# Encoder block on one core: second MLP product with sums in kept PSUM banks, weight sums by adding transfers, and a second level of Strassen's scheme in chunks 2 to 4

## The chip, the core and the metric

One core of a Trainium2 chip runs the whole layer as one program. The core has TensorE (PE in the profile; PEld is its weight load), VectorE (DVE), ScalarE (ACT), GpSimd (POOL) and SyncE (SP, which here only issues transfers). The metric is the device time of one execution in microseconds (us); lower is better. Before the change it is 1208.2 us, the median of 3 runs (1207.58 to 1208.48).

## What is computed

The reference is one layer of a bidirectional encoder on 1024 tokens of width 1024, in float32. The change touches only the last line, the second product of the MLP:

```python
def reference(x, norm1_g, w_in, ..., norm2_g, w_mlp_in, w_mlp_out):
    ...
        x = x + merged @ w_o[l]
        h = rms_norm(x, norm2_g[l]) @ w_mlp_in[l]
        x = x + jnp.square(jax.nn.relu(h)) @ w_mlp_out[l]
    return x
```

`w_mlp_out` has 4096 rows and 1024 columns.

## The kernel before

**Precision and Strassen's scheme.** Each float32 operand is scaled by a power of two and split into two float16 parts, a high one (ACT writes it) and a low one (DVE: operand times scale minus high part). A product takes three passes: high by high, high by low, low by high (`PASSES`). Both MLP products use Strassen's scheme in Winograd's form, in which the 2 x 2 block product takes seven products of sums of blocks instead of eight; the sums of blocks are made in float32 before the split.

**Chunks and products.** The second MLP product runs over four chunks `s` of the inner dimension. A chunk has seven products `o` = 0 to 6, so that 28 products `n = 7 * s + o` follow each other; their operands are numbered `i = 16 + n`. The table `ORDER` (L1713) says which of the seven formed blocks of h and which weight block product `o` takes: w11, t2, w21, t3, t1, t4, w22, where t2 is w12 + w22 + w11 (the signs are in the stored weights), t4 is t2 + w21, t1 is w11 + w12 and t3 is w12 + w22. The blocks of h come from DRAM (`HS`, loaded by `h_load` into four turns of `hf`). A product gives 512 tokens by 512 columns. It is done in four units `j` of 128 tokens, each a PSUM bank filled by 12 matmuls of 512 columns (four inner tiles by three passes).

**Preparation.** `prep2(s)` is a Python generator in the list `bg`: each call issues the next few instructions. It first takes the sums of squares of the weights (L1730, L1733, on ACT), makes t2 on POOL (L1739, L1740), and works out the scale: `sum_of` and `scale_of` use a matmul with ones and a chain of tiny DVE instructions ("the scale chain"). Then, for each product, it waits in the order of issue until `pe_done` says that product i - 3 is issued (`gate`), takes one of three operand buffers `OPS[i]`, and issues ACT's high part and DVE's low part of h (L1765, L1767, 2048 elements a partition) and of the weights (L1770, L1776, 1024 elements, twice). After product 0 POOL makes w11 + w12 in place (L1781), after product 1 w12 + w22 (L1785), after product 3 t2 + w21 (L1789). After product 4 the raw weights of the next chunk are loaded and `prep2(s + 1)` joins the list.

**Where results go.** Banks come from `anybank`, which turns through all eight. Products 0, 1 and 3 are added into three accumulators `acc` (chunk 0 by ACT, L1864; later ones by DVE, L1866), the others straight into the result `X1` (DVE, L1875; product 4 into two places). In the last chunk `combine` adds the accumulators to each other and to `X1`, on DVE and POOL, and each finished 128 x 512 block of `X1` is stored.

**What sets the order.** The order of each engine's queue is the order in which the Python code issues: `unit` (L207) issues 12 matmuls, then the eviction `post` of the unit before (`settle`), then calls `step` and `tick` a given number of times (here 2 and 4), and each tick draws one step from the generators. An engine runs its queue in that order; semaphores are added where data needs them. So an eviction of DVE stands behind whatever preparation was issued ahead of it, and a matmul that needs the bank waits for that eviction. The text counts chunks from 1 to 4 (`s` = 0 to 3) and products from 0 to 6.

## Time and profile before

| What | Value |
|---|---|
| Runs, median of 3 | 1208.2 us |
| Profiled execution, span from the first to the last instruction | 1205.3 us |
| Mean granted clock of PE | 1.000 |
| Second MLP product on PE | 911.1 to 1201.3 us |
| PE busy over the span | 99% |
| DVE / ACT / POOL busy over the span | 78% / 63% / 36% |
| Bytes moved by transfers | 173.36 MB, mean 144 GB/s |

The profile is one execution on the chip. A row of a group gives the source line, engine, operation, output and inputs, shape, count, busy time and the mean duration of one, then the engine's idle time just before and what ended it. A row of the timeline gives start, duration, engine, line and operation, with idle time in brackets. Matmuls overlap: what a unit costs is the distance from start to start. The chunks start about 911.1, 983.7, 1056.2 and 1128.8 us.

### The profile page before, as it was taken

The numbers are of one execution on the slowest core, as the hardware profiler recorded it, in microseconds if no ns is written. First come the engines' busy times: TensorE is split into PE (matmuls) and PEld (weight loads), VectorE is DVE, ScalarE is ACT, GpSimd is POOL, SyncE is SP. The second block draws the span as 40 slices with busy tenths as digits, with TensorE's granted clock in tenths as the row PEclk, the third lists the DMA queues.
The fourth block names the chain that finished last, engine by engine and source line by source line (L and its number), as shares of the span: only waits on it lengthen the run. The fifth ranks groups of instructions, "written<-read, shape, count | busy, mean of one in ns | idle before, by whom it ended". The sixth has DMA issues, their size and how long they took to land.

```text
span 1205.3 us, 17076 instructions
## 1 busy us (share of the span) xinstructions
PE 1188.0 (99%) x6294; PEld 573.8 (48%) x6294; DVE 938.7 (78%) x1759; ACT 759.8 (63%) x1183; POOL 433.1 (36%) x280
## 2 busy tenths in 40 slices
PE   6999999999999999999999999999999999999998
PEld 4444445555444444444467444444444444444444
DVE  7777988988368787877878655545548999999997
ACT  7766679867554545337779778678676744746440
POOL 1640011222311112001004465565567471553662
PEclk9999999999999999999999999999999999999999
DMA  7766657676542211224386545445465925334202
GB/s 264 151 213 141 140 119 130 133 146 123 103 123 65 67 56 53 70 93 187 57 155 183 182 159 192 149 139 193 145 247 201 352 97 217 129 138 194 105 35 105
DMA packets 171012, 173.36 MB, mean 144 GB/s; under 512 B 131504, under 2 KB 132016, under 8 KB 166832
## 3 DMA queue, kind: packets, MB, share of 16 engines
q1 hardware_dynamic: 170352, 168.07, 47.9%
q10 hardware_dynamic: 576, 4.19, 0.8%
q8 instruction: 49, 0.80, 0.3%
q14 instruction: 35, 0.29, 0.1%
HBM read 102.51 MB, written 37.75 MB: 116 GB/s over the span
## 4 chain that ended last, share of the span: by engine, by line
PE 73%; DVE 9%; ACT 1%; issue 1%; DMA 1%; DVEq 0%; ACTq 0%
PE ps_d L210 26%; PE ps_s L210 23%; PE ps_o L210 16%; PE ps_d L1039 6%; DVE w_s L1163 2%; PE ps_o L1016 1%; PE ps_s L959 1%; DVE sg L1279 1%; DVE P L999 1%; DMA u2T<-v 1%; DVE sz L973 1%; ACT w_s L1167 0%; DVE sc L317 0%; DVE m L1281 0%; ACT sg L1245 0%
## 5 line engine op out<-in xcount | busy, mean ns | idle before, releaser
L210 PEld LDWEIGHTS <-ops 128*128 128x128 f16 x1356 | 132.4, 98 | 157.3
L210 PEld LDWEIGHTS <-w 128*128 128x128 f16 x1368 | 132.8, 98 | 140.0 <-DMA u2T<-v 0.6
L1039 PE MATMUL ps_d<-uT,w_ws 128*128 128x512 f16 x528 | 123.7, 379 | 0.1
L210 PE MATMUL ps_d<-ops 128*128 128x512 f16 (+1 forms) x528 | 118.3, 374 | 0.0
L1765 ACT ACTIVATE ops<-hf,sc 128x2048 f16<-128x2048 f32 x26 | 52.0, 2000 | 97.9 <-PE ps_o L210 35.2
L210 PE MATMUL ps_s<-ops 128*128 128x512 f16 x492 | 112.9, 379 | 0.0
L1152 POOL TENSOR_TENSOR tsum<-raw 128x512 f32<-128x512 f32 x28 | 46.0, 1658 | 149.6 <-ACT raw L1138 141.6
L1345 POOL TENSOR_TENSOR as<-as 128x512 f32<-128x512 f32 x56 | 77.5, 1384 | 39.3 <-ACT as L1625 36.0
L210 PEld LDWEIGHTS <-w_s 128*128 128x128 f16 x588 | 56.8, 98 | 69.4 <-DVE w_s L1163 1.9
L210 PE MATMUL ps_d<-u2x,w 128*128 128x512 f16 (+1 forms) x360 | 80.0, 372 | 0.0
L210 PEld LDWEIGHTS <-uT 128*128 128x128 f16 x504 | 49.0, 98 | 59.6 <-DMA uT<-u 0.8
L1039 PEld LDWEIGHTS <-w_ws 128*128 128x128 f16 x528 | 51.2, 98 | 54.5 <-DVE cv L861 0.4
L210 PE MATMUL ps_o<-ops 128*128 128x512 f16 x336 | 77.1, 379 | 0.0
L1767 DVE SCALAR_TENSOR_TENSOR ops<-hf,sc,ops 128x2048 f16<-128x2048 f32 x26 | 74.0, 2846 | 3.7 <-ACT ops L1765 3.7
L210 PE MATMUL ps_o<-u2T,w 128*128 128x512 f16 (+1 forms) x324 | 71.7, 371 | 0.0
L1138 ACT ACTIVATE raw<-raw,sc 128x256 f32<-128x256 f32 x172 | 71.0, 493 | 0.8 <-DMA raw<-in_weights 0.7
L1152 POOL TENSOR_TENSOR gsum<-raw 128x512 f32<-128x512 f32 x14 | 19.0, 1376 | 133.0 <-issue 72.8
L1167 ACT ACTIVATE w<-raw,sc 128x512 f16<-128x512 f32 (+1 forms) x28 | 24.6, 927 | 54.1 <-DVE sc L426 54.1
L297 DVE SCALAR_TENSOR_TENSOR w_ws<-raw,sc,w_ws 128x512 f16<-128x512 f32 (+2 forms) x72 | 51.2, 763 | 4.7 <-ACT w_ws L306 4.7
L1658 DVE TENSOR_TENSOR as<-ps_d,as 128x512 f32<-128x512 f32 (+1 forms) x14 | 9.4, 672 | 55.8 <-ACT as L1677 53.4
L210 PE MATMUL ps_s<-u2T,w 128*128 128x512 f16 (+1 forms) x252 | 52.7, 359 | 0.0
L982 ACT ACTIVATE sz<-sz,sc 128x384 f32<-128x384 f32 (+1 forms) x64 | 37.2, 582 | 22.5 <-DVE sc L973 15.0
(357 smaller groups left out, 2629.5 us busy)
## 6 DMA issues: line engine op xcount, KB each, us to landing
raw<-in_weights SPq DMA_DIRECT2D x88, 512.0 KB, 5.4
hs<-as SPq DMA_DIRECT2D x16, 1792.0 KB, 8.7
hf<-hs SPq DMA_DIRECT2D x26, 1024.0 KB, 6.3
w2x<-in_weights SPq DMA_DIRECT2D x16, 512.0 KB, 8.1
raw<-in_weights SPq DMA_DIRECT2D x16, 384.0 KB, 3.5
xt<-in_x SPq DMA_DIRECT2D x8, 512.0 KB, 10.0
gs<-s ACTq DMA_DIRECT2D x4, 1024.0 KB, 4.0
x<-in_x SPq DMA_DIRECT2D x8, 512.0 KB, 9.8
```

The lines of the kernel that those rows point to most:

```text
L210: T.matmul(ps, l, r, start=a, stop=b)
L297: V.scalar_tensor_tensor(lo, self.raw[p][:, o:o + m], sc[:, c:c + 1], hi, op0=OP.mult, op1=OP.subtract)
L959: T.matmul(ps[:, :nb * 128], QD[:, p, e, w, i * 128:(i + 1) * 128], KD[:, 2 * p + e, lo * 128:(lo + nb) * 128], start=w == 0, stop=w == 1)
L982: A.activation(z, z, AF.Exp, scale=-1.0, bias=sc[:, d["mx"]], accum_out=sc[:, d["sm"]])
L1039: T.matmul(ps, l, r, start=a, stop=b)
L1138: A.activation(v, v, AF.Copy, scale=sc[:, at(g, 4 * i + k)])
L1152: G.tensor_tensor(t[:, o], a, b, op=OP.add)
L1163: V.scalar_tensor_tensor(o(1), w, sc[:, s], o(0), op0=OP.mult, op1=OP.subtract)
L1167: A.activation(o(0), w, AF.Copy, scale=sc[:, s])
L1345: sub.tensor_tensor(z[o], z[a], z[b], op=op)
L1765: A.activation(P[:, 1, 0], hf, AF.Copy, scale=sc[:, Rs])
L1767: V.scalar_tensor_tensor(P[:, 1, 1], hf, sc[:, Rs], P[:, 1, 0], op0=OP.mult, op1=OP.subtract)
```

## The change

**Kept banks.** Four of the eight banks (`chain`) belong to the units `j` of products 0, 1, 3 and 5. Product 0 starts a bank, products 1, 3 and 5 add into it without clearing it, and after each of them DVE adds or subtracts the bank's sum so far into its place in `X1` (`PLACE`, with the scale `inv` or its negative `neg`). The accumulators and `combine` are gone. The other four banks (`fixed`) turn for products 2, 4 and 6 and the scale chain's matmul.

**Adding transfers.** In chunks 2 to 4 t2 starts as a second load of w12 from DRAM (two loads of 512 KB) and the sums of weights are transfers issued on POOL's queue that add their source to their destination in SBUF (`accum_op`), each 512 KB; ten in a chunk. Chunk 1 keeps POOL's sums.

**A second level.** In chunks 2 to 4 product 2 (h's block 1 with w21) is split once more: `deep_prep` forms seven blocks of 256 x 256 on either side, in place in `hf` and `w2x`, with sums on POOL and DVE, and splits them into high and low parts in one tile `deep` of its own. `deep_units` does seven sub-products with 2 x 6 matmuls of 256 columns, in pairs, each ahead of one unit of product 3, in three of the `fixed` banks, some of which gather several sub-products. Product 2 needs no gate and no operand buffer.

```diff
@@ -71,14 +71,16 @@
     rc = [0]
+    fixed = []
+
     def anybank():
         rc[0] += 1
-        return bank("dsodsods"[rc[0] % 8])
-
-
-    sc = base.tile([128, 512], F32, name="sc")
+        return fixed[rc[0] % len(fixed)] if fixed else bank("dsodsods"[rc[0] % 8])
+
+
+    sc = base.tile([128, 520], F32, name="sc")
     sci = sc.bitcast(I32)
-    area = {"keep": [0, 0, 144], "prep": [144, 144, 240], "tmp": [240, 240, 512]}
+    area = {"keep": [0, 0, 144], "prep": [144, 144, 240], "tmp": [240, 240, 512], "neg": [512, 512, 520]}
     def cols_of(kind, n):
         a = area[kind]
@@ -204,10 +206,10 @@
         V.tensor_scalar(sc[:, out], bk[:, 0:1], floor, None, op0=OP.max)
         yield
-    def unit(mms, post=None, steps=0, ticks=0):
+    def unit(mms, post=None, steps=0, ticks=0, free=False):
         for ps, l, r, a, b in mms:
-            T.matmul(ps, l, r, start=a, stop=b)
+            T.matmul(ps, l, r, start=a, stop=b, skip_group_check=free)
         units[0] += 1
         work[0] += len(mms) * mms[0][0].shape[-1]
         settle()
@@ -1639,7 +1641,7 @@
             m = tmp()
             V.tensor_reduce(sc[:, m], sc[:, bsum[q // 4]], axis=AX, op=OP.max)
             yield
-            yield from pow2(m, 14, *R[q // 4])
+            yield from pow2(m, 13, *R[q // 4])
             r_ready[q // 4] = True
     def quad(q, c0=0, c1=512):
@@ -1735,9 +1737,25 @@
             yield
         sums = sum_of(sm)
         T2 = later["t2"]()
-        for i in range(2):
-            G.tensor_tensor(T2[:, i], w12[i], w22[i], op=OP.add)
-            G.tensor_tensor(T2[:, i], T2[:, i], w11[i], op=OP.add)
+
+        def add(o, w):
+            for i in range(2):
+                if s == 0:
+                    G.tensor_tensor(o[i], o[i], w[i], op=OP.add)
+                else:
+                    G.dma_start(o[i], w[i], accum_op=OP.add)
+
+        t2 = [T2[:, i] for i in range(2)]
+        if s == 0:
+            for i in range(2):
+                G.tensor_tensor(t2[i], w12[i], w22[i], op=OP.add)
+                G.tensor_tensor(t2[i], t2[i], w11[i], op=OP.add)
+        else:
+            for i in range(2):
+                load_into(t2[i], c2[s], 2 + i)
+            yield
+            add(t2, w22)
+            add(t2, w11)
         yield
         if s == 0:
             yield from gate(17)
@@ -1747,20 +1765,25 @@
         sw, inv = yield from scale_of(sums, 0)
         fw = keep()
         mul(iR, sw, fw)
-        c2[s].inv = inv
+        c2[s].inv, c2[s].neg = inv, cols_of("neg", 1)
+        V.tensor_scalar(sc[:, c2[s].neg], sc[:, inv], -1.0, None, op0=OP.mult)
         yield
         for o, (f, name) in enumerate(ORDER):
             n = 7 * s + o
             i = 16 + n
-            yield from gate(i)
+            if name != "w21" or s not in DEEP:
+                yield from gate(i)
             pool, tag = TAGS[i % 3]
-            if n > 1:
+            if n > 1 and (name != "w21" or s not in DEEP):
                 OPS[i] = pool.tile([128, 2, 2, 2048], F16, name="ops", tag=tag)
-            P = OPS[i]
             while ("h", n) not in later:
                 yield
             if 1 < n < 25:
                 h_load(n + 3)
+            if name == "w21" and s in DEEP:
+                yield from deep_prep(i, later.pop(("h", n)), X2[s][:, 0:2], Rs, fw)
+                continue
+            P = OPS[i]
             hf = later.pop(("h", n)).rearrange("p k t -> p (k t)")
             A.activation(P[:, 1, 0], hf, AF.Copy, scale=sc[:, Rs])
             yield
@@ -1777,16 +1800,15 @@
                 yield
             ready.add(i)
             if name == "w11":
-                for i2 in range(2):
-                    G.tensor_tensor(w11[i2], w11[i2], w12[i2], op=OP.add)
+                add(w11, w12)
                 yield
             elif name == "t2":
-                for i2 in range(2):
-                    G.tensor_tensor(w12[i2], w12[i2], w22[i2], op=OP.add)
+                add(w12, w22)
+                if s in DEEP:
+                    add(t2, w21)
                 yield
-            elif name == "t3":
-                for i2 in range(2):
-                    G.tensor_tensor(T2[:, i2], T2[:, i2], w21[i2], op=OP.add)
+            elif name == "t3" and s not in DEEP:
+                add(t2, w21)
                 yield
             elif name == "t1":
                 done[0] += 4
@@ -1794,6 +1816,103 @@
                 if s < 3:
                     w2x_load(s + 1)
                     bg.append(prep2(s + 1))
+            yield
+
+    DEEP = (1, 2, 3)
+    HSLOT, WSLOT = {0: 0, 1: 1, 3: 2, 5: 3, 6: 4, 2: 5, 4: 6}, {0: 0, 1: 1, 2: 2, 3: 3, 6: 4, 4: 5, 5: 6}
+
+    def deep_prep(i, hf, wx, sh, sw):
+
+        t = OPS[i] = w5p.tile([128, 2, 2, 7, 512], F16, name="deep")
+        w4 = wx.rearrange("p a (k c) -> p (a k) c", c=512)
+        src = [v.rearrange("p k (h c) -> p k h c", h=2) for v in (hf, w4)]
+
+        def todo(m, part):
+            v, o = src[m], t[:, m]
+            if part == 0:
+                return v[:, :, 0], [o[:, w, 0:2].rearrange("p f (k c) -> p (f k) c", k=2) for w in range(2)]
+            if part == 1:
+                return v[:, 2:4, 1], [o[:, w, 2].rearrange("p (k c) -> p k c", k=2) for w in range(2)]
+            return v, [o[:, w, 3:7].rearrange("p f c -> p (f c)").rearrange("p (h k c) -> p k h c", h=2, k=4)
+                       for w in range(2)]
+
+        scale = (sh, sw)
+
+        def hi(m, part):
+            v, o = todo(m, part)
+            A.activation(o[0], v, AF.Copy, scale=sc[:, scale[m]])
+
+        def lo(m, part):
+            v, o = todo(m, part)
+            if part < 2:
+                V.scalar_tensor_tensor(o[1], v, sc[:, scale[m]], o[0], op0=OP.mult, op1=OP.subtract)
+            else:
+                for k in range(4):
+                    V.scalar_tensor_tensor(o[1][:, k], v[:, k], sc[:, scale[m]], o[0][:, k],
+                                           op0=OP.mult, op1=OP.subtract)
+
+        def q(m, h, k):
+            return src[m][:, 2 * k:2 * k + 2, h]
+
+        hi(0, 0), hi(0, 1)
+        yield
+        lo(0, 0), lo(0, 1)
+        yield
+        a, b = (lambda h, k: q(0, h, k)), (lambda k, c: q(1, c, k))
+        G.tensor_tensor(a(0, 0), a(0, 0), a(1, 0), op=OP.subtract)
+        G.tensor_tensor(a(1, 0), a(1, 0), a(1, 1), op=OP.subtract)
+        V.scalar_tensor_tensor(a(1, 1), a(0, 0), -1.0, a(1, 1), op0=OP.mult, op1=OP.subtract)
+        G.tensor_tensor(a(0, 1), a(0, 1), a(1, 1), op=OP.add)
+        yield
+        hi(1, 0), hi(1, 1)
+        yield
+        lo(1, 0)
+        yield
+        lo(1, 1)
+        yield
+        for o, x, y in ((b(0, 0), b(0, 0), b(0, 1)), (b(0, 1), b(0, 1), b(1, 1)), (b(1, 1), b(0, 0), b(1, 1)),
+                        (b(1, 0), b(1, 0), b(1, 1))):
+            V.tensor_tensor(o, x, y, op=OP.add)
+            yield
+        hi(0, 2)
+        yield
+        hi(1, 2)
+        yield
+        lo(0, 2)
+        yield
+        lo(1, 2)
+        ready.add(i)
+        yield
+
+    def deep_units(s):
+
+        t, inv, neg = OPS.pop(16 + 7 * s + 2), c2[s].inv, c2[s].neg
+        banks = {m: anybank() for m in "abc"}
+        seq = {1: ("a", 1, 0, 0, inv), 5: ("c", 1, 1, 1, inv), 2: ("b", 1, 0, 0, inv), 6: ("a", 0, 0, 1, neg),
+               3: ("c", 0, 0, 1, inv), 7: ("a", 0, 1, 1, neg), 4: ("a", 0, 1, 0, inv)}
+
+        def sub(m):
+            bk, fresh, h, c, g = seq[m]
+            ps, (f, w) = banks[bk], SEVEN[m]
+            mms = []
+            for j in range(2):
+                o = ps[:, 256 * j:256 * j + 256]
+                for n, (k, (sa, sw)) in enumerate((k, p) for k in range(2) for p in PASSES):
+                    at_h, at_w = 256 * k + 128 * j, 256 * k
+                    mms.append((o, t[:, 0, sa, HSLOT[f], at_h:at_h + 128], t[:, 1, sw, WSLOT[w], at_w:at_w + 256],
+                                n == 0 and j == 0 and fresh == 1, n == 5))
+
+            def post():
+                x = X1[:, 2 * h:2 * h + 2, 256 * c:256 * c + 256]
+                V.scalar_tensor_tensor(x, ps.rearrange("p (j c) -> p j c", j=2), sc[:, g], x, op0=OP.mult, op1=OP.add)
+                if m == 4 and s == 3:
+                    for r in range(4):
+                        SP.dma_start(out[128 * r:128 * r + 128, :512], X1[:, r, :512])
+            unit(mms, post, 1, 2, True)
+
+        for ms in (1, 5), (2, 6), (3, 7), (4,):
+            for m in ms:
+                sub(m)
             yield
     def first2():
@@ -1820,67 +1939,52 @@
     p4.close()
     p5 = ExitStack()
     w5p = later["pool"] = p5.enter_context(tc.tile_pool(name="p5", bufs=1, reuse_waits="tile"))
-    acc = {i: w5p.tile([128, 4, 512], F32, name=f"acc{i}") for i in (1, 6, 7)}
     t2 = w5p.tile([128, 2, 1024], F32, name="t2")
     later["t2"] = lambda: t2
     later["junk"] = w5p.tile([128, 2048], BF16, name="junk")
-    combined = set()
-    PLACE = {2: ((0, 0),), 4: ((4, 512), (0, 512)), 5: ((4, 0),), 6: ((0, 512),)}
-    SUM = {0: 1, 1: 6, 3: 7}
-
-    def combine(j, o):
...
+    PLACE = {0: ((0, 0, 1),), 1: ((0, 512, 0),), 2: ((0, 0, 1),), 3: ((4, 512, 0),), 4: ((4, 512, 1), (0, 512, 1)),
+             5: ((4, 0, 1),), 6: ((0, 512, 1),)}
+    LAST = {2: (0, 0), 4: (4, 512), 5: (4, 0), 6: (0, 512)}
+    eight = [anybank() for _ in range(8)]
+    chain = eight[:4]
+    fixed[:] = eight[4:]
+
+    def step2(n, j):
+        s, o = n // 7, n % 7
+        P, c = OPS[16 + n], c2[s]
+        bk = chain[j] if o in (0, 1, 3, 5) else anybank()
+        for c0, m in ((0, 256), (256, 256)) if n == 27 and j == 3 else ((0, 512),):
+            ps = bk[:, c0:c0 + m]
+
+            def post(ps=ps, c0=c0, m=m):
+                for b, d, plus in PLACE[o]:
+                    t = X1[:, b + j, d + c0:d + c0 + m]
+                    V.scalar_tensor_tensor(t, ps, sc[:, c.inv if plus else c.neg], t, op0=OP.mult, op1=OP.add)
+                if s == 3 and o in LAST:
+                    b, d = LAST[o]
+                    r = (b + j) * 128
+                    SP.dma_start(out[r:r + 128, d + c0:d + c0 + m], X1[:, b + j, d + c0:d + c0 + m])
+
+            mms = group(ps, [(P[:, 1, sa, 512 * k + 128 * j:512 * k + 128 * j + 128],
+                              P[:, 0, sw, 512 * k + c0:512 * k + c0 + m]) for k in range(4) for sa, sw in PASSES])
+            if o in (0, 1, 3, 5):
+                mms = [(p, l, r, a and o == 0, b) for p, l, r, a, b in mms]
+            unit(mms, post, 2, 4, o in (0, 1, 3, 5))
     for n in range(28):
         s, o = n // 7, n % 7
+        if o == 2 and s in DEEP:
+            continue
         need(16 + n)
...
+        side2 = iter(())
+        if o == 3 and s in DEEP:
+            need(15 + n)
+            side2 = deep_units(s)
         for j in range(4):
+            next(side2, None)
+            step2(n, j)
+        OPS.pop(16 + n)
         pe_done[0] = 17 + n
     settle()
     p5.close()
```

43 lines of the change are left out of this document (removed).

## The prediction

> **What bounds the kernel now.** Read first: the head of the page, then the busy time of each engine in four windows, one for each chunk of the second MLP product (the only part that the diff touches).
>
> ```profile
> PE 1188.0 (99%) x6294; PEld 573.8 (48%) x6294; DVE 938.7 (78%) x1759; ACT 759.8 (63%) x1183; POOL 433.1 (36%) x280
> ...
> 911.10:983.70 72.60, 72.60 (x339) 32.91 (x338) 63.99 (x59) 50.50 (x50) 41.83 (x15) 1.00 0.64 239
> 983.70:1056.20 72.50, 72.50 (x338) 32.88 (x337) 69.43 (x63) 37.51 (x33) 33.38 (x11) 1.00 0.43 158
> ...
> 1128.80:1201.30 72.50, 72.50 (x349) 33.89 (x347) 68.58 (x63) 20.41 (x15) 36.20 (x17) 1.00 0.21 80
> ```
>
> The columns after a window are its length and the busy time of PE, PEld, DVE, ACT and POOL, then granted clock, DMA share and GB/s. PE is busy the whole window at clock 1.00: every microsecond that PE gains or waits here is a microsecond of the kernel. DVE, at 64 to 69 of 72.5 us, is close behind. The timeline of PE says what one unit (12 matmuls into one bank) takes, and when the chunk's first two products start:
>
> ```profile
> 911.12 2.75 PE L210 MATMUL ps_s<-ops 128*128 128x512 f16 x12
> 913.71 2.75 PE L210 MATMUL ps_o<-ops 128*128 128x512 f16 x12
> ...
> 921.48 2.75 PE L210 MATMUL ps_d<-ops 128*128 128x512 f16 x12
> ...
> 654.36 1.47 PE L210 MATMUL ps_d<-u2x,mH 128*128 128x256 f16 x12
> 655.67 1.47 PE L210 MATMUL ps_s<-u2x,raw 128*128 128x256 f16 x12
> ```
>
> Start to start, a unit of 512 columns takes 913.71 - 911.12 = 2.59 us, one of 256 columns 1.31. A product is four units, 10.36 us; product 1 of chunk 1 starts at 921.48.
>
> **The matmuls removed.** In chunks 2 to 4 product P2's four units of 512 columns become seven sub-products of 12 matmuls with 256 columns: 7 x 1.31 = 9.17 us for 10.36, 1.19 less, times 3: **-3.6 us**. That is all the gain on the path that sets the end.
>
> **DVE's work.** Its pace where nothing disturbs it, and where POOL adds at the same time:
>
> ```profile
> 1002.28 2.34 DVE L1767 SCALAR_TENSOR_TENSOR ops<-hf,sc,ops 128x2048 f16<-128x2048 f32 x1
> 1004.54 2.47 DVE L1776 SCALAR_TENSOR_TENSOR ops<-raw,sc,ops 128x1024 f16<-128x1024 f32 x2
> 1006.93 0.74 DVE L1866 SCALAR_TENSOR_TENSOR acc<-ps_o,sc,acc 128x512 f32<-128x512 f32 x1
> 1007.59 0.74 DVE L1866 SCALAR_TENSOR_TENSOR acc<-ps_d,sc,acc 128x512 f32<-128x512 f32 x1
> ...
> 1030.79 6.68 DVE L1776 SCALAR_TENSOR_TENSOR ops<-w2x,sc,ops 128x1024 f16<-128x1024 f32 x2
> ...
> 881.46 5.33 POOL L1345 TENSOR_TENSOR as<-as 128x512 f32<-128x512 f32 x4 [12.72 <-ACT as L1625]
> ```
>
> A low part of h costs 2.26 us, the two of a weight 2.39, an eviction 0.66. Beside POOL's sums the pair takes 6.68, so the sums that become transfers give DVE back up to 4.2 us a pair. A chunk with a second level then asks of DVE: six ordinary products 6 x 4.65 = 27.9; the second level's low parts, 2 x 3584 elements, and five sums of 512 at 0.6 each (half of 1.2): 8.4 + 3.0; 28 + 7 evictions 23.1; the scale chain 1. That is 63.4 of PE's 71.3 us. On the average DVE is not the bound, and the relief is worth nothing by itself: PE never waited for DVE. What counts is where DVE is late.
>
> **The kept banks, chunk 1.** Before, eight banks rotated, and products 0, 1 and 3 of chunk 1 went to their accumulators by ACT. Now product 1 adds into the four banks of product 0, so its first matmul waits until DVE has read bank 0 into x1. In the changed program's order that read is queued behind both low parts of product 2's weights. In the trace of before that stretch of DVE's queue is:
>
> ```profile
> 921.13 2.34 DVE L1767 SCALAR_TENSOR_TENSOR ops<-hf,sc,ops 128x2048 f16<-128x2048 f32 x1
> 926.82 0.16 DVE L1640 TENSOR_REDUCE sc<-sc 128x1 f32<-128x4 f32 x1 [3.35 <-ACT as L1625]
> 927.08 2.13 DVE L1776 SCALAR_TENSOR_TENSOR ops<-w2x,sc,ops 128x1024 f16<-128x1024 f32 x1
> ...
> 929.20 2.23 DVE L1776 SCALAR_TENSOR_TENSOR ops<-w2x,sc,ops 128x1024 f16<-128x1024 f32 x1
> 931.35 0.14 DVE L112 TENSOR_SCALAR sc<-sc 128x1 int32<-128x1 int32 x1
> ...
> 918.78 2.00 ACT L1765 ACTIVATE ops<-hf,sc 128x2048 f16<-128x2048 f32 x1 [4.21 <-DMA hf<-hs]
> ...
> 924.69 2.00 ACT L1625 ACTIVATE as<-as,sc 128x2048 f32<-128x2048 f32 x1
> ```
>
> Nothing ahead of it is changed: ACT starts after the load of h, squares the last quad of the first MLP product, DVE's maximum waits for that until 926.82, and the low parts end at 931.35. The read follows, 0.74 us, and PE goes on at about 932.1 where it wants 921.48: **+10.6 us**. The other three reads follow at 0.66 each, while PE takes 2.59 a unit, so it waits once.
>
> **The second level's preparation, chunks 2 to 4.** I walk DVE's queue as the changed program orders it, with zero where product 5 of the chunk ahead ends on PE. Product 6 then runs to 10.4, product 0 to 20.7, product 1 should start there. Chunk 3: the scale chain ends at 3.9 (product 6's first unit ends at 2.6, its eviction at 3.4, four scalars follow); then low parts of product 0 and evictions to 9.9; of product 1 to 14.5; eviction 15.2; second level, h, first 1536 elements 1.8 us to 17.0; bank 0 of product 0 read at 17.7; two dependent sums on POOL (5.33 / 4 = 1.33 each) end at 19.7, DVE's own sum at 20.3; second level, weight 22.1; bank 1 read 22.8; four sums of weights 25.2; bank 2 read 25.8; eight low parts of 512, 4.8 us, 30.6; bank 3 read 31.3. PE wants bank 3 at 28.5: a wait of 2.8. Behind it stand product 3's low parts (35.9), four evictions and product 4's h (40.8), then the read of the first sub-product (41.5), whose bank the fourth sub-product wants at 40.4: 1.1 more. Chunk 4 has the same order: 3.9 us each. In chunk 2 product 0's low parts come one eviction earlier; its walk has bank 0 at 20.8 and bank 1, behind the eight low parts, at 26.3 where PE wants 23.4: 3.0. Together **+10.8 us**.
>
> **The adding transfers.** No such transfer is in the trace; the nearest are plain ones:
>
> ```profile
> w2x<-in_weights SPq DMA_DIRECT2D x12, 512.0 KB, 7.7
> raw<-in_weights SPq DMA_DIRECT2D x11, 512.0 KB, 5.7
> out_y<-x SPq DMA_DIRECT2D x15, 256.0 KB, 2.1
> out_y<-x SPq DMA_DIRECT2D x2, 128.0 KB, 1.7
> ```
>
> (KB each, us to landing.) 128 KB more cost 0.4 us, so 512 KB alone take some 2.9, a pair 4.5; in a crowd 7.7. Each is issued on POOL's queue, in order, and the next pair waits where it needs the one before. Three pairs (w11, w12, then t2 with w21) stand between product 0's low parts (9.2) and DVE's in-place sums of w21 (22.8), which must not start before t2 has read w21; behind them on DVE stand the reads for which PE waits. At 4.5 a pair the last lands at 22.7: nothing. At 7.7 it lands at 32.3, 9.5 us late in each chunk, 28.5 in all. Below nothing it can't go: the reads stay where they are. I take 3 us a chunk, nearer to the low end because the DMA share of these windows is under one half: **+9 us**. The load of t2 and its two adding pairs, 5.7 + 2 x 7.7 = 21.1 us, fit the 23 us between product 5's low part (-15.3) and ACT's use (8); the first pair's slack is 2 us, so POOL's issue time isn't free either.
>
> The Trainium skill (DMA: Bandwidth & Descriptors, "Anatomy of one DMA — SWDGE (gpsimd) path") gives 2.0 us plus bytes over 436 GB/s for a transfer issued there: 3.2 us for 512 KB, an estimate by that page; no run here shows one, and by it this term would be 0 to 1 us a chunk.
>
> **Edits at nothing.** The constant 13 for 14, the wider sc and one more tensor_scalar a chunk (0.15 us as the rows of scalars show). Gone in chunk 4 are 12 sums on POOL and 12 on DVE; evictions of chunk 1 move from ACT to DVE, where the walk has them. SP gets two more loads of 512 KB a chunk. The end itself stays: the last bank in two halves, evicted and stored.
>
> ```profile
> 1198.69 2.78 PE L210 MATMUL ps_d<-ops 128*128 128x256 f16 x24
> 1201.51 0.88 DVE L1875 SCALAR_TENSOR_TENSOR x<-ps_d,sc,x 128x256 f32<-128x256 f32 x2 [1.87 <-PE ps_d L210]
> ```
>
> **Sum:** -3.6 + 10.6 + 10.8 + 9 = +26.8. The profiled span is 1205.3 us, the median of the runs 1208.2, so 2.9 lie around the span; after: span 1232, run **1235 us**, 2.2% slower.
>
> **Rivals.** (a) *Only the first chunk waits.* DVE without POOL's sums reaches the later reads in time: 1208.2 - 3.6 + 10.6 = 1215.2. For it: 6.68 us against 2.47 for the same pair. Against it: the walk already uses the quick pace, and its waits come from the order. (b) *The transfers decide.* Pairs at 7.7 us: 1208.2 + 17.8 + 28.5 = 1254.5. For it: three pairs in a row on one queue; against it: little else moves then. (c) *Twice that*, because a destination is read and written: 3 x 15.4 against 13.6 us of room, 32.6 late a chunk, 98 in all: 1324. (d) *Not slower:* the reads of the kept banks are done before PE asks, in chunk 1 before 921.48, because ACT's square and the low parts of product 2 come 10.6 us sooner, and DVE keeps ahead later for the same reason: 1208.2 - 3.6 = 1204.6. It decides as soon as bank 0 is free within the four units of product 0. For it: POOL's sums slowed the low parts at 929 to 931; against it: only 2 of the 10.6 us are such slowing, the rest is a load and ACT.
>
> The Trainium skill (SBUF — State Buffer, "Who interferes with whom") has the port pair that VectorE and GpSimd share as an exclusive lock, and descriptors that GpSimd writes held up while VectorE has it; the 6.68 us row agrees with the lock. Held-up descriptors would be a cause of (b).
>
> **How the numbers follow.** Forecast 0.56, with a range of its own of 1222 to 1246; (a) 0.14, (b) 0.17, (c) 0.06, (d) 0.07. The range 1214 to 1268 takes in (a) and (b) and leaves out (c), (d) and little of the rest. 0.2% is 2.4 us, about what can be told from no change: faster has (d)'s chance but for 0.01, 0.06; same 0.02, a mix of (a) and (d); slower 0.92.
>
> **What would show it.** In the profile after: PE with idle time of some 10 us before the first matmul of product 1 in chunk 1, released by DVE's eviction; about 3 to 7 us before product 1 in each of chunks 2 to 4, released by the same line; units of the second level 1.31 us apart; adding transfers of 3 to 8 us on POOL's queue. PE without a gap near 921 would break the largest term; gaps of over 15 us ahead of product 1 in chunks 2 to 4, with DVE waiting for a transfer, would mean (b) or (c).

## The result, and the profile after

| What | Before | After |
|---|---|---|
| Runs, median | 1207.9 us (4 runs, 1207.0 to 1208.5) | 1253.7 us (4 runs, 1251.6 to 1254.7) |
| Profiled execution, span | 1205.3 us | 1252.0 us |
| Mean granted clock of PE | 1.000 | 0.985 |
| Second MLP product, units of product 0 of chunk 1 to the end | 911 to 1201 us | 911 to 1248 us |
| POOL busy | 433 us | 349 us |

The changed kernel is slower: ratio 1.038, 95% interval 1.0365 to 1.0394. The forecast was 1235 with a range of 1214 to 1268; the time lies inside the range, 19 us above the forecast. The span has grown by 46.7 us, and all the rows below are about where these went.

First the head of the page of the changed kernel: PE's busy time, and PE and its granted clock in 40 slices of 31 us (a 9 is 90% or more).

```profile
PE 1195.5 (95%) x6402; PEld 586.1 (47%) x6402; DVE 926.4 (74%) x1814; ACT 761.5 (61%) x1180; POOL 348.9 (28%) x277
...
PE   6999999999999999999999999999969979979798
...
PEclk9999999999999999999999999999979989989899
```

Before, PE was full in every slice but the first and the last. Now it has holes in the last quarter, and, which the prediction had not thought of, the clock dips in the same slices. PE's busy time is 7.5 us longer although 3 x 1.19 us of matmuls were taken out. Next the waits of PE from 900 us on (what it waited for: us in total, times, longest):

```profile
PE ps_o L212 <- DVE x L1963: 15.6, 3, 7.2
PE ps_s L212 <- DVE x L1963: 11.1, 3, 8.1
PE ps_s L212 <- issue: 10.9, 1, 10.9
PE ps_s L212 <- DVE x L1907: 1.5, 2, 0.7
```

L1963 is DVE's eviction, and in these rows the read of a kept bank; L1907 is the eviction of a sub-product. Together 39.1 us: 10.9 in chunk 1 (the row with "issue" is that one; the timeline shows below that it too ends with the read), 28.2 in chunks 2 to 4. The timeline of PE shows where they stand, here in chunks 1 and 3 (start, duration, in brackets the idle time before and what ended it):

```profile
932.41 5.19 PE L212 MATMUL ps_s<-ops 128*128 128x512 f16 x12 [10.90 <-issue]
937.44 2.75 PE L212 MATMUL ps_o<-ops 128*128 128x512 f16 x12
...
1100.07 4.99 PE L212 MATMUL ps_o<-ops 128*128 128x512 f16 x12 [7.08 <-DVE x L1963]
1104.90 2.75 PE L212 MATMUL ps_d<-ops 128*128 128x512 f16 x12
1109.47 2.75 PE L212 MATMUL ps_s<-ops 128*128 128x512 f16 x12 [1.82 <-DVE x L1963]
...
1119.68 1.47 PE L212 MATMUL ps_s<-deep 128*128 128x256 f16 x12 [0.74 <-DVE x L1907]
```

In chunk 1 product 1's first unit starts 10.9 us late; in chunk 3 (and in chunk 4) its first unit is on time and the second one, which adds into the second kept bank (ps_o), starts 7.1 us late. And the first unit behind each of these waits takes 937.44 - 932.41 = 5.03 and 1104.90 - 1100.07 = 4.83 us in place of 2.59. The same units with their granted clock (windows of the trace; the column after POOL's is the clock):

```profile
932.41:937.44 5.03, 5.03 (x12) 1.73 (x13) 5.03 (x5) 0.00 (x0) 4.95 (x4) 0.51 0.43 160
937.44:942.60 5.16, 5.16 (x25) 2.35 (x24) 5.16 (x3) 0.00 (x0) 3.34 (x1) 1.00 1.05 306
```

Twelve matmuls at clock 0.51 behind the wait, then 1.00 again. In chunks 2 to 4 the unit behind the long wait takes 4.56, 4.83 and 5.07 us, so the four cost 2.44 + 1.97 + 2.24 + 2.48 = 9.1 us more than full speed. Sum: -3.6 + 39.1 + 9.1 = 44.6 of the 46.7 us. Of the other 2.1 us, 1.3 are in the way of counting: a wait counts from the end of a unit, 2.75 us after its start, while a unit without a wait costs 2.59, which makes 0.16 for each of eight waits. 0.4 is in the second unit of chunk 4 (3.14 us in place of 2.75), and 0.4 at two sub-products.

What DVE does ahead of the read in chunk 1 is as forecast:

```profile
927.05 0.16 DVE L1642 TENSOR_REDUCE sc<-sc 128x1 f32<-128x4 f32 x1 [3.65 <-ACT as L1627]
...
929.43 2.22 DVE L1799 SCALAR_TENSOR_TENSOR ops<-w2x,sc,ops 128x1024 f16<-128x1024 f32 x1
...
931.58 0.74 DVE L1963 SCALAR_TENSOR_TENSOR x<-ps_s,sc,x 128x512 f32<-128x512 f32 x1
```

The read ends at 932.32, PE goes on at 932.41. In chunk 3 the order on DVE is the forecast one too, but it holds a wait that the forecast didn't have. DVE's waits for POOL in the three chunks (us in total, times, longest), and DVE's timeline in chunk 3:

```profile
DVE hf L1864 <- POOL hf L1863: 26.0, 3, 8.8
```

```profile
1086.45 0.75 DVE L1963 SCALAR_TENSOR_TENSOR x<-ps_s,sc,x 128x512 f32<-128x512 f32 x1
1095.81 0.69 DVE L1864 SCALAR_TENSOR_TENSOR hf<-hf 128x512 f32<-128x512 f32 x1 [8.61 <-POOL hf L1863]
...
1099.28 0.74 DVE L1963 SCALAR_TENSOR_TENSOR x<-ps_o,sc,x 128x512 f32<-128x512 f32 x1
```

and POOL's in the same stretch, where DMA_DIRECT2D is the issue of an adding transfer:

```profile
1083.57 0.86 POOL L1746 DMA_DIRECT2D raw<-w2x  x1 [3.59 <-DMA raw<-raw]
1087.77 0.86 POOL L1746 DMA_DIRECT2D raw<-w2x  x1 [3.34 <-DMA raw<-raw]
1088.38 1.17 POOL L1746 DMA_DIRECT2D t<-w2x  x1
1092.27 0.87 POOL L1746 DMA_DIRECT2D t<-w2x  x1 [2.72 <-issue]
1092.83 1.60 POOL L1862 TENSOR_TENSOR hf<-hf 128x512 f32<-128x512 f32 x1
1094.51 1.26 POOL L1863 TENSOR_TENSOR hf<-hf 128x512 f32<-128x512 f32 x1
```

POOL has two short sums of h to make, L1862 and L1863, and DVE stands 8.6 us for them, from 1087.2 to 1095.8. The sums themselves take 2.9 of these. They are late because they stand behind the issues: those of raw<-w2x had waited 3.59 and 3.34 us for raw<-raw to land, and the last issue of t<-w2x was held another 2.72 us, for which the trace names no cause. The bank that PE wants at about 1093.0 is read from 1099.28 on, behind DVE's sum.

### The profile page after: what moved, and what is told of

It reads as the page before. It is cut to its first block, busy times and chain, and to the rows that moved or that the text cites. A ratio compares the mean times of both kernels' runs of the same rounds, so it can differ in the third digit from the quotient of the medians.

```text
span 1252.0 us, 17392 instructions
## 1 busy us (share of the span) xinstructions
PE 1195.5 (95%) x6402; PEld 586.1 (47%) x6402; DVE 926.4 (74%) x1814; ACT 761.5 (61%) x1180; POOL 348.9 (28%) x277
## 4 chain that ended last, share of the span: by engine, by line
PE 45%; DVE 11%; issue 8%; DMA 6%; POOL 4%; ACT 2%; SPq 0%; POOLq 0%; DVEq 0%; ACTq 0%
PE ps_d L212 18%; PE ps_s L212 16%; PE ps_o L212 11%; DMA t<-in_weights 2%; DVE w_s L1165 2%; DMA t<-raw 1%; DVE ops L1790 1%; DMA raw<-raw 1%; DVE deep L1851 1%; POOL as L1347 1%; DMA hf<-hs 1%; POOL t L1746 1%; DVE x L1963 1%; DVE sg L1281 1%; DMA u2T<-v 1%
## 5 line engine op out<-in xcount | busy, mean ns | idle before, releaser
L212 PEld LDWEIGHTS <-ops 128*128 128x128 f16 x1212 | 120.2, 100 | 184.4 <-issue 53.1
L212 PE MATMUL ps_s<-ops 128*128 128x512 f16 x492 | 116.3, 389 | 22.0 <-DVE x L1963 11.1
L1788 ACT ACTIVATE ops<-hf,sc 128x2048 f16<-128x2048 f32 x23 | 45.8, 1993 | 83.7 <-PE ps_s L212 57.2
L212 PE MATMUL ps_d<-ops 128*128 128x512 f16 (+1 forms) x420 | 93.5, 374 | 0.0
L212 PE MATMUL ps_o<-ops 128*128 128x512 f16 x300 | 73.6, 398 | 15.6 <-DVE x L1963 15.6
L1790 DVE SCALAR_TENSOR_TENSOR ops<-hf,sc,ops 128x2048 f16<-128x2048 f32 x23 | 55.7, 2422 | 5.2 <-ACT ops L1788 5.2
```

Source lines behind the costliest of these rows:

```text
L212: T.matmul(ps, l, r, start=a, stop=b, skip_group_check=free)
L1788: A.activation(P[:, 1, 0], hf, AF.Copy, scale=sc[:, Rs])
L1790: V.scalar_tensor_tensor(P[:, 1, 1], hf, sc[:, Rs], P[:, 1, 0], op0=OP.mult, op1=OP.subtract)
```

## The experiments

All times are device medians; the kernel before was run beside each group, with 1207.5, 1206.9, 1207.6 and 1207.5 us in the four. All kernels in the table compute the whole layer.

| Run | What differs | us | ratio to before (95%) |
|---|---|---|---|
| after | the change | 1253.7 | 1.038 (1.0365 to 1.0394) |
| e_first_read | chunk 1: reads ahead of product 2's low parts | 1248.0 | 1.0332 (1.0317 to 1.0348) |
| e_no_second | no second level | 1220.3 | 1.0101 (1.0084 to 1.0118) |
| e_h_sums_dve | sums of h on DVE | 1247.1 | 1.0326 (1.031 to 1.0341) |
| e_w21_dram | t2 + w21 taken from DRAM, later | 1242.3 | 1.0282 (1.0266 to 1.0297) |
| e_w21_h | the last two together | 1232.2 | 1.0225 (1.0198 to 1.0252) |
| e_reads_no_second | no second level, reads of chunk 1 first | 1208.4 | 1.0011 (1.0002 to 1.002) |
| e_h_early | all repairs, half for h early | 1214.9 | 1.0067 (1.0052 to 1.0082) |
| e_pool_sums | weight sums on POOL again | 1267.0 | 1.0496 (1.0481 to 1.0512) |
| e_paced | e_h_early with the rest later | 1206.1 | 0.9989 (0.998 to 0.9998) |
| e_paced_evenly | e_paced with other pauses | 1206.9 | 0.9995 (0.9986 to 1.0004) |
| e_waits_a, e_waits_b | e_reads_no_second with idle sums on DVE | 1219.0, 1226.6 | 1.0095 (1.008 to 1.011), 1.016 (1.0143 to 1.0177) |

**Chunk 1's wait.** The low part of product 2's h, and with it that of its weights, waits in chunk 1 until product 1's first unit is issued, so the four reads are queued ahead of it.

```diff
+            while i == 18 and units[0] < start5[0] + 5:
+                yield
             V.scalar_tensor_tensor(P[:, 1, 1], hf, sc[:, Rs], P[:, 1, 0], op0=OP.mult, op1=OP.subtract)
```

> Edit: in chunk 1 the low parts of product 2 are issued behind the eviction of product 0's units, so that DVE reads the kept banks first. Theory (the order of DVE's queue makes the wait): the 10.9 us wait ahead of product 1 in chunk 1 goes, and with it the slow unit behind it (5.03 us for 2.59): 13.3 us less, 1240.5, at most some 5 us of it given back because chunk 2 is reached sooner than its weights: 1240 to 1246. Rival (DVE has too much to do and the backlog only moves on): 1249 or more, with a wait as long in chunk 1's later products.

It took 1248.0 us, a gain of 5.8, between the expected 1240 to 1246 and the rival's 1249, so neither came out. PE's wait in chunk 1 fell from 10.9 to 4.1 us and not to nothing. DVE's timeline in that run says why:

```profile
926.15 0.16 DVE L1642 TENSOR_REDUCE sc<-sc 128x1 f32<-128x4 f32 x1 [3.25 <-ACT as L1627]
...
926.60 0.74 DVE L1965 SCALAR_TENSOR_TENSOR x<-ps_s,sc,x 128x512 f32<-128x512 f32 x1
```

L1642 is the maximum over the last quad of the first MLP product, and it waits 3.3 us for ACT's square. Its result is the scale of h in chunk 4, but the read stood behind it. The unit after the 4.1 us still took 5.07 us, so almost nothing of the slow start was saved either.

**The second level as a whole.** It is left out of all chunks (product 2 is an ordinary product again); kept banks and transfers stay.

```diff
-    DEEP = (1, 2, 3)
+    DEEP = ()
```

> Edit: no second level, product 2 is ordinary in all chunks; kept banks and adding transfers stay. Theory (the long waits of chunks 2 to 4 come from the second level's preparation; chunk 1's wait from the kept banks): only chunk 1's 13.3 us stay against the kernel before: 1221, no wait of over 1 us in chunks 2 to 4. Rival (kept banks or the adding transfers by themselves hold PE in every chunk): waits of 5 us or more ahead of product 1 in chunks 2 to 4, 1235 or more.

1220.3 us, as expected of the theory: the second level costs 1253.7 - 1220.3 = 33.4 us net of the matmuls it saves, and what is left, 12.8 us over before, is one wait of PE of 10.1 us in chunk 1 and the slow unit behind it (5.07 us). To settle that nothing else is in it, the edit of e_first_read was added to this kernel, and the reads were put ahead of the maximum too:

```diff
+            while q == 15 and units[0] < start5[0] + 7:
+                yield
             m = tmp()
             V.tensor_reduce(sc[:, m], sc[:, bsum[q // 4]], axis=AX, op=OP.max)
```

> Kept banks and adding transfers without the second level, and in chunk 1 the reads of the kept banks are put ahead of product 2's low parts and ahead of the maximum over the last quad of the first MLP product, whose queue place made DVE wait 3.3 us for ACT in the run with early reads alone. Theory 1 (without the second level the only cost is chunk 1's wait of 10.1 us and the slow unit behind it): 1207 to 1210.5 us, about the time of the kernel before; DVE's low parts of product 1 end at about 922.9, so PE waits some 1 us there. Rival (kept banks or adding transfers cost something elsewhere as well): 1213 us or more, with a wait of PE in chunks 2 to 4.

1208.4 us, PE waiting 0.3 us in the whole second product. With the reads in that place, kept banks and adding transfers by themselves are within 0.2% of the kernel before, and chunk 1's wait 1220.3 - 1208.4 = 11.9 us.

**What DVE waits for in chunks 2 to 4.** Two suspects stand in POOL's queue: the sums of h, behind the transfers, and the transfers themselves, one of which (t2 + w21) must have read w21 before DVE may change it. Each was taken away alone. First the three sums of h, from POOL to DVE:

```diff
-        G.tensor_tensor(a(0, 0), a(0, 0), a(1, 0), op=OP.subtract)
-        G.tensor_tensor(a(1, 0), a(1, 0), a(1, 1), op=OP.subtract)
+        V.tensor_tensor(a(0, 0), a(0, 0), a(1, 0), op=OP.subtract)
+        V.tensor_tensor(a(1, 0), a(1, 0), a(1, 1), op=OP.subtract)
         V.scalar_tensor_tensor(a(1, 1), a(0, 0), -1.0, a(1, 1), op0=OP.mult, op1=OP.subtract)
-        G.tensor_tensor(a(0, 1), a(0, 1), a(1, 1), op=OP.add)
+        V.tensor_tensor(a(0, 1), a(0, 1), a(1, 1), op=OP.add)
```

> Edit: the three sums of h's blocks at the second level move from POOL to DVE. Theory (two things are late one behind the other: POOL's sums, which stand behind the transfers in POOL's queue, and the transfer that reads w21, which lands about when DVE's sums of w21 begin now): DVE's 8.6 us wait for POOL goes, but most of it comes back ahead of the sums of w21: 1243 to 1254. Rival (only POOL's queue is late): 7.2 + 2.3 us less in each of three chunks, 1225.

1247.1 us, 6.7 less. DVE's longest sum of waits is now another one (L1875 are the in-place sums of w21):

```profile
DVE w2x L1875 <- DMA t<-w2x: 16.9, 6, 4.6
```

The wait for POOL, 26.0 us in the changed kernel, is gone, and 16.9 us of waiting for the transfer that reads w21 have come out from under it. Then the other one alone: the sum of t2 with w21 reads w21 from DRAM, where DVE doesn't change it, and is issued after product 3's split.

```diff
             elif name == "t3":
-                if s in DEEP:
-                    add(t2, w21)
+                if s in DEEP:
+                    for i2 in range(2):
+                        G.dma_start(t2[i2], bass.AP(tensor=weights.tensor, offset=weights.offset + c2x[s].offs[i2],
+                                                    ap=[[1024, 128], [1, 1024]]), accum_op=OP.add)
```

> Edit: w21 is added to t2 from DRAM, after product 3's split, so that no transfer reads the w21 that DVE changes in place and two transfers fewer stand ahead of POOL's sums of h. Theory (order of POOL's queue and the wait for w21): the waits ahead of product 1 in chunks 2 to 4 shrink from about 9 to 3 to 4 us, and the slow unit behind each goes: some 7.5 us less in each, 1231, within 5. Rival (the adding transfers are slow by themselves, or DVE is): the same 9 us of waits, 1250 or more.

1242.3 us, between the two expected numbers. POOL's sums of h are now behind two transfers fewer, but still behind w12 + w22, and DVE's waits say so (first the wait that is left in this run):

```profile
DVE hf L1867 <- POOL hf L1866: 10.7, 3, 4.1
```

**Both together.**

> Both edits on POOL's queue together: the sum of t2 with w21 reads w21 from DRAM and is issued after product 3's split, and the three sums of h are made by DVE. With the first alone (1242.3 us) DVE still waited 10.7 us in all, in 3 places, for POOL's sum of h. Theory 1 (the waits ahead of product 1 in chunks 2 to 4 are DVE's reads queued behind preparation that itself waits for POOL): most of these 10.7 us go, less some 2 us a chunk that the sums now cost DVE: 1231 to 1238 us. Rival (DVE's own work ahead of the reads is what lasts; POOL is only late beside it): no gain over 1242.3, so 1241 to 1247 us, the same waits at the same places.

1232.2 us (1231.7 to 1238.3), inside the expected 1231 to 1238: 6.7 and 11.5 us alone, 21.6 together. PE's waits alone don't explain that the two make more than their sum: they fell by 5.0 and 12.4 us, and by 16.7 together. The rest lies in the slow units: alone, four were left in either kernel (7.5 and 8.3 us over full speed, 9.1 in the changed kernel), together two (3.9 us), since two of the three waits of 3.1 to 3.2 us here were followed by units of full speed. PE's waits in this run:

```profile
PE ps_s L212 <- issue: 10.9, 1, 10.9
PE ps_s L212 <- DVE x L1966: 6.9, 3, 3.2
PE ps_o L212 <- DVE x L1966: 3.1, 1, 3.1
PE ps_d L212 <- DVE x L1966: 0.8, 2, 0.4
PE ps_s L212 <- DVE x L1910: 0.7, 1, 0.7
```

Chunk 1's is as before; chunks 2 to 4 have 6.9 + 3.1 + 0.8 + 0.7 = 11.5 us left. That is what DVE's own order costs when it waits neither for POOL nor for a transfer.

**Transfers or POOL.** The reverse test: the weight sums of chunks 2 to 4 go back to POOL, with the second level in place.

```diff
-                if s == 0:
-                    G.tensor_tensor(o[i], o[i], w[i], op=OP.add)
-                else:
-                    G.dma_start(o[i], w[i], accum_op=OP.add)
+                G.tensor_tensor(o[i], o[i], w[i], op=OP.add)
```

> The changed kernel with the weight sums on POOL in all chunks, as before the change, in place of the adding transfers. Theory 1 (what delays DVE is that POOL's sums of h stand behind the weight sums in POOL's queue, and a pair of sums on POOL takes longer, 5.3 us and more, than issuing its two transfers): the wait of DVE for POOL's sum of h grows from 8.6 us, and DVE is slowed beside POOL as well: 1260 to 1285 us. Rival (the landing of the adding transfers, 7.2 us in the median, is the delay): faster than the changed kernel, 1230 to 1248 us.

1267.0 us, in the expected interval, though only one half of the reason came true. DVE's wait for POOL's sum of h didn't grow; it fell from 26.0 to 12.4 us in all, where no landing of a transfer stands in POOL's queue. DVE beside POOL is slower, as its timeline in chunk 3 shows, and is busy 960.6 us in this run, 926.4 in the changed kernel:

```profile
1087.13 6.65 DVE L1796 SCALAR_TENSOR_TENSOR ops<-t,sc,ops 128x1024 f16<-128x1024 f32 x2
...
1094.36 5.45 DVE L1845 SCALAR_TENSOR_TENSOR deep<-hf,sc,deep 128x1024 f16<-128x1024 f32 x2
```

The same two rows of the changed kernel:

```profile
1081.54 2.48 DVE L1799 SCALAR_TENSOR_TENSOR ops<-t,sc,ops 128x1024 f16<-128x1024 f32 x2
...
1084.59 1.94 DVE L1848 SCALAR_TENSOR_TENSOR deep<-hf,sc,deep 128x1024 f16<-128x1024 f32 x2
```

The pair takes 6.65 us beside POOL's sums and 2.48 beside the transfers, the other 5.45 and 1.94. So the transfers do what they are for, and replacing POOL's sums is worth 13.3 us in this kernel.

**A version without the waits.** DVE has nothing to do while the scale chain waits; the second level's half for h needs no scale of the weights. It is issued there, at most three steps of it, with the repairs above:

```diff
+            if r == WAIT and s in DEEP and taken < 3:
+                taken += 1
+                advance(side_h)
```

> All repairs together: early reads in chunk 1 as in the kernel without the second level, w21 for t2 from DRAM, the sums of h on DVE, and the second level's half for h issued up to three steps while the scale chain still waits (DVE has nothing else there), with the remaining low parts cut in two. Theory 1 (the second level costs by its place in DVE's queue, not by its amount): waits ahead of product 1 in chunks 2 to 4 of at most 5 us each and no slow units behind the short ones: 1206 to 1216 us. Rival (DVE has too little time in these chunks, so the waits only move): 1225 us or more.

1214.9 us, inside the expected 1206 to 1216. The largest part of what is left, about half of it, is one wait of 3.0 us in chunk 2 with its slow unit, which was not expected behind so short a wait. DVE's timeline there, and behind it PE's:

```profile
987.92 0.75 DVE L1991 SCALAR_TENSOR_TENSOR x<-ps_o,sc,x 128x512 f32<-128x512 f32 x1
...
995.01 2.14 DVE L1905 TENSOR_TENSOR w2x<-w2x 128x512 f32<-128x512 f32 x3
997.06 0.74 DVE L1991 SCALAR_TENSOR_TENSOR x<-ps_s,sc,x 128x512 f32<-128x512 f32 x1
```

```profile
997.95 4.27 PE L212 MATMUL ps_s<-ops 128*128 128x512 f16 x12 [3.01 <-DVE x L1991]
1002.67 2.75 PE L212 MATMUL ps_o<-ops 128*128 128x512 f16 x12 [0.45 <-DVE x L1991]
```

The eviction at 987.92 belongs to a unit that PE had finished by 979.4: DVE's evictions run many microseconds behind, because preparation that isn't due yet (the sums of w21 are for sub-products that start at 1010) is issued between them. So that half is issued later, and the sub-products that gather in one bank are set further apart:

```diff
+        for _ in range(4):
+            yield
         hi(1, 0), hi(1, 1)
...
         hi(1, 2)
         yield
+        for _ in range(8):
+            yield
...
-        for ms in (1, 5), (2, 6), (3, 7), (4,):
+        for ms in (1, 5), (2,), (6, 3), (7,), (4,):
```

> The kernel with the second level's half for h early (1214.9 us), and two things more. The weights' half of the second level is issued later: four steps of pause ahead of it and eight ahead of its last low parts, so that DVE's reads of product 0's kept banks are queued ahead of it (in that kernel they still ran up to 12 us behind PE). And the sub-products go 1 and 5, 2, 6 and 3, 7, then 4 behind product 3's last unit, so that two that gather in one bank are further apart. Theory 1 (only queue places are left, 9 us of waits and slow units): PE waits under 1 us in chunks 2 to 4, and the 3.6 us of matmuls saved show: 1204 to 1207 us, 1 to 4 below the kernel without the second level (1208.4). Rival (DVE at some 68 of 71 us a chunk has no room left, waits move to products 3 to 6): 1210 us or more.

> As the run before, with pauses of four steps at each of three places: ahead of the weights' half, ahead of its sums, and ahead of its last low parts. Theory 1: the same, 1204 to 1207.5 us; which of the two is shorter isn't foreseen within 1 us. Rival (no room left on DVE): 1210 us or more, with waits of PE ahead of product 3 where the later preparation ends too late.

1206.1 us for the first, inside the expected 1204 to 1207, and 1.5 below the kernel before beside it: ratio 0.9989, 0.998 to 0.9998, a gain at the edge of what can be told. The second, with its pauses spread evenly, took 1206.9 us, also as expected, and can't be told from before (0.9995, 0.9986 to 1.0004). First the head of e_paced's page, then PE's waits in it:

```profile
PE 1184.3 (98%) x6402; PEld 583.8 (48%) x6402; DVE 927.4 (77%) x1823; ACT 761.3 (63%) x1180; POOL 338.9 (28%) x268
```

```profile
PE ps_s L212 <- DVE x L1995: 1.0, 1, 1.0
PE ps_s L212 <- issue: 0.3, 1, 0.3
```

With 1.3 us of waits left, PE's busy time is 3.7 us below the 1188.0 of before: the matmuls saved, at last to be seen.

**The slow unit by itself.** In the kernel without the second level, idle sums of 512 were put on DVE ahead of the first read of product 0's banks in chunks 2 to 4 (4, 6 and 11 of them in one kernel, 5, 8 and 16 in the other).

```diff
+                if o == 0 and j == 0:
+                    for k in range(EXTRA.get(s, 0)):
+                        V.tensor_tensor(idle[:, 1 + k % 3], idle[:, 0], idle[:, 0], op=OP.add)
```

> A measurement of the slow unit by itself: the kernel without the second level (1208.4 us, no wait of PE over 0.3 us), with 4, 6 and 11 idle sums of 512 on DVE (0.66 us each) ahead of the first read of product 0's banks in chunks 2, 3 and 4. That read ended at 993.7 in chunk 2, and PE wants the bank at 994.1, so PE should wait some 2.3, 3.6 and 6.9 us, with nothing of the second level there. Theory 1 (a wait of PE of some 3 us or more is itself followed by a unit of 12 matmuls that takes 4.2 to 5.2 us in place of 2.6): the unit behind the first wait is normal, those behind the second and third are slow; time 1208.4 + 12.8 + about 4.5 = 1225.7. Rival (the slow units come of what else ran in those kernels, the adding transfers late in the chunk or DVE's and ACT's work on the second level): units of 2.6 us behind all three, 1221 us.

> As the run before, with 5, 8 and 16 idle sums: waits of some 3.0, 4.9 and 10.2 us. Theory 1: slow units behind the second and third at least, and the third costs no more than the second (one unit, about 2.4 us), so 1208.4 + 18.1 + 5 to 7 = 1231.5 to 1233.5. Rival (no slow unit without the second level): 1226.5 us; or, if the slowing grows with the wait, more than one slow unit behind the 10.2 us.

The waits came out shorter than planned, and with them the times (1219.0 and 1226.6). Clearing the idle sums' tile (1.76 us of DVE) stood ahead of the read in chunk 1 and made PE wait 2.4 us there, with a slow unit behind it; PE came that much later to the next chunks, so that part of the delay made for them fell into this room. The times alone therefore decide nothing, although they lie near the rival's 1221 and 1226.5; the unit behind each wait does. In e_waits_a the wait in chunk 4 was 3.88 us and the unit behind it took 3.85; in e_waits_b a wait of 2.08 us in chunk 3 was followed by a unit of full speed. In e_waits_b, PE's timeline and its clock in chunk 4:

```profile
1153.59 4.76 PE L212 MATMUL ps_s<-ops 128*128 128x512 f16 x12 [6.89 <-DVE x L1973]
1158.18 2.75 PE L212 MATMUL ps_o<-ops 128*128 128x512 f16 x12
```

```profile
1153.59:1158.18 4.59, 4.59 (x12) 1.62 (x13) 4.59 (x5) 0.00 (x0) 0.00 (x0) 0.55 0.00 0
1158.18:1163.30 5.12, 5.12 (x25) 2.35 (x24) 3.29 (x4) 0.00 (x0) 0.00 (x0) 1.00 0.00 0
```

A slow unit at clock 0.55 with no second level, no transfer in flight (the last two columns, DMA share and GB/s, are 0) and ACT and POOL idle: the rival, that the slowness comes of what else ran, falls. One unit is slow, and the next at full clock.

## Why the prediction was right in kind and 19 us short

In the span the forecast is 46.7 - 26.8 = 19.9 us short: 9.1 in slow units, 7.7 in the term of the transfers, 0.3 in chunk 1 and 0.7 in DVE's walk, and the 2.1 us of small things above.

**The matmuls, -3.6: right.** The sub-products start 1.31 us apart, and where the waits are gone the 3.7 us show in PE's busy time.

**Chunk 1, +10.6: right, with its mechanism.** The wait was 10.9 us; the read came at 931.58 where the working had 931.35. Undone by moving the read in DVE's queue, it gave back 11.9 in the kernel without the second level; what the term lacked is the slow unit behind the wait.

**DVE's walk in chunks 2 to 4, +10.8: right as an account of DVE's own queue.** With POOL and the transfers out of its way PE's waits there are 11.5 us. Chunk for chunk they are 3.6, 3.6 and 4.3 (the waits over 0.3 us in that run's timeline), the walk had 3.0, 3.9 and 3.9. The places agree too: 3.1 us ahead of the second kept bank in chunk 2 and 3.2 ahead of the fourth in chunks 3 and 4, as the walk had them.

**The adding transfers, +9: the mechanism right, the size too small, and one place missed.** Waits of 28.2 us in chunks 2 to 4 less the 11.5 of DVE's own order leave 16.7 us where the term had 9. The mechanism that was priced, DVE's in-place sums waiting until the transfer has read w21, is real: with POOL's sums out of the way it made DVE wait 16.9 us, 5.6 a chunk, between the ends 0 and 9.5 and above the 3 taken. The step that failed is the sentence in the walk "two dependent sums on POOL (5.33 / 4 = 1.33 each) end at 19.7". They cost 1.6 and 1.3 us, near the price, but they were taken to start when DVE was ready, while the change puts the issues of w11 + w12, w12 + w22 and t2 + w21 ahead of them in POOL's queue. With the walk's zero at 1069.52 in chunk 3, where product 6 starts on PE, DVE's read of bank 0 ends at 17.7, as forecast; POOL's second sum ends at 26.2 and not at 19.7. Of what held the queue, the trace names the landing of raw<-raw for the second pair; for the last issue of the third pair, held 2.7 to 4.0 us a chunk, it names nothing, so that part of the cause stays open (us in total, times, longest):

```profile
POOL t L1746 <- issue: 10.1, 3, 4.0
```

The landing was dearer than the low end of the bounds, too. The issues of the second product after (KB each, median us to landing):

```profile
t<-w2x POOLq DMA_DIRECT2D x12, 512.0 KB, 7.3
t<-raw POOLq DMA_DIRECT2D x6, 512.0 KB, 4.8
raw<-raw POOLq DMA_DIRECT2D x6, 512.0 KB, 6.2
raw<-w2x POOLq DMA_DIRECT2D x6, 512.0 KB, 8.1
```

The three kinds that stand ahead of the sums of h (6.2, 8.1 and 7.3) are nearer to the 7.7 us of the crowd than to the 4.5 of the quiet pair; only t<-raw, earlier in the chunk, is not. The Trainium skill (DMA: Bandwidth & Descriptors, "Anatomy of one DMA — SWDGE (gpsimd) path") would give 3.2 us each; the trace doesn't agree for these adding transfers.

**Slow units, not in the sum: 9.1 us.** The prediction took a wait as its length. Behind each of four waits of 7 us and more the next unit took 2.0 to 2.5 us longer, at a granted clock of 0.51 in the one shown above. This is the largest single part of the error, and no term of the sum stood for it. The Trainium skill (TensorE: Matmul & The Clock Gate, "Part 1: The HAM clock gate (the "warmup" mystery)") has the rule: half clock after an idle window of about 3.4 us, full again after as long of work, with windows that run freely. The trace agrees in the halving (0.51) and in one unit being slow. By the Trainium skill's figures, an estimate, 1.7 us (half of 3.4) would have been added to the forecast for chunk 1's wait, the only one that it put above 3.4 us at a stretch.

**Edits at nothing.** SP's additional loads and the longer scale chain cost nothing that can be seen: the kernel with all of them and no second level takes 1208.4. But "the relief is worth nothing by itself" can hold only for the order before; in the changed order POOL's sums cost 13.3 us more. The exclusive lock that the prediction took from the Trainium skill (SBUF — State Buffer, "Who interferes with whom") agrees with the 6.65 us against 2.48; the held-up descriptors that it named as a cause of (b) were not seen: an issue took 0.85 to 1.2 us, and through all three of the longer holds DVE stood idle.

**The rivals.** (b), the transfers decide, named 1254.5 and the run took 1253.7, but the agreement is partly chance: beside the 17.8 us that it shares with the forecast (18.8 measured), it had 28.5 us of landings alone, while the runs show 16.7 for landings and POOL's queue together, 9.1 for the clock and 2.1 of small things. (a) fell with the 28.2 us of waits in chunks 2 to 4, (c) with transfers of 4.8 to 8.1 us in the median, (d) with the read at 931.58. From 1253.7 to 1206.1 the steps of the runs are 21.6 us (POOL's queue and w21), then 17.3 (chunk 1's reads and the half for h early, not tried one by one in that kernel), then 8.8 (the rest later).

## What to carry to other kernels

Short work that another engine waits for must not be queued behind instructions that wait for a transfer; look in each queue for what stands ahead of it, also on an engine that is idle most of the time. Where banks are kept, the reads become part of PE's path: issue preparation that isn't due behind them, and price a wait of PE of more than about 2 us at its length plus a slow unit. A wait can hide under another: when DVE's 26.0 us of waiting for POOL were taken away, 16.9 us of waiting for a transfer came out, so take both away before calling either cheap.

## What the runs showed of the hardware that was not expected

**The clock after a wait.** In the second MLP product of all profiled executions of this study, 23 units of 12 matmuls of 512 columns came behind a wait of PE of 3.88 us or more, and all took 3.8 to 5.3 us in place of 2.59. Behind waits of 2.1 us or less none was slower than 2.75. Between 2.2 and 3.3 us both are found, 8 slow ones of 11, even for the same length; in e_w21_h two waits of 3.21 us were followed by

```profile
1094.21 4.36 PE L212 MATMUL ps_s<-ops 128*128 128x512 f16 x12 [3.21 <-DVE x L1966]
...
1171.11 2.75 PE L212 MATMUL ps_s<-ops 128*128 128x512 f16 x12 [3.21 <-DVE x L1966]
```

That equal waits end either way would fit the free-running window of the Trainium skill, but no run here tests that. A wait of 2.2 us was enough (3.94 us for the unit behind it, in e_first_read, though a longer wait had ended 7 us before it), and one of 2.35 us with no other wait ahead of it in this product (4.28 us, in e_waits_a, chunk 1); the 3.4 us that the Trainium skill gives for an idle window are more than either. Beyond that the penalty doesn't grow with the wait: 10.9 us and 4.1 us of waiting cost 5.03 and 5.07 us for the unit.

**POOL's issue of an adding transfer** takes 0.86 us as a rule, and up to 1.17. The last one ahead of the sums of h, behind three others of 512 KB, was held 2.7 us with no releaser in the trace (1092.27 above; 10.1 us in three places in all), while DVE stood idle. What holds it is open.
